# 33 instead of 30 seven-product sets in the down projection of a hybrid decoder layer, with other places for its sums and PSUM banks

## The chip, the cores and the metric

The kernel runs on one core of a Trainium2 chip. The metric is the device time of one execution in microseconds. Times "by the median" are those of the runs without a profile; the profile is of one further execution, whose own time is given beside its span. TensorE (PE) multiplies, VectorE (DVE) and ScalarE (ACT) work on tiles, SyncE (SP) issues most transfers, GpSimd (POOL) some early ones.

## The reference

One decoder layer on 256 tokens of width 2048: a norm, one input projection into attention heads and pooling channels, both mixers, an output projection with a residual, a second norm, and a gated MLP of hidden width 5632. All of it is float32. The part that matters here is the last product:

```python
gate, val = jnp.split(y, 2, axis=-1)
return (jax.nn.silu(gate) * val) @ w_down
```

`silu(gate) * val` has 256 x 5632 elements (44 blocks of 128 along the hidden width), `w_down` is 5632 x 2048, and the result is added to the residual x.

## The kernel before

**Precision.** Every float32 factor is split into a high part `wh` (rounded to the fp32r type by ScalarE, line 180) and a low part `wl` (what is left, `raw - wh`, by VectorE, line 186). A product of two split factors is three matmuls: high by high, high by low, low by high.

**Rows.** All weights come as a list of rows (`rows`, from `plan`). A row is one transfer into a `raw` tile of up to 128 x 2048, a high part and a low part. The rows are used in the order of the list; the steps of the program, u, are the halves of a row, or whole rows of the two special kinds below. At the first step of a row c the program issues, in this order: the high part of row c + 3 (ScalarE), the low part of row c + 2 (VectorE), a `make` if one is due, work set for this step by `later`, work that the step before left in `deferred`, and then the matmuls of row c. Each engine works strictly in the order in which its instructions are issued. `raw` tiles rotate over five buffers, `wh` over four, `wl` over three. When the low part of a row is done its `raw` tile is free, and the transfer five places further on in the list is issued on SP's queue.

**MLP stages.** The MLP is done in three thirds of the hidden width (`THIRDS`: 8, 8 and 6 pairs of 128 x 2 hidden channels). In each third an up stage makes the hidden values, a gate block and a value block of 16 half rows together for every pair, and then a down stage multiplies them by `w_down`. A down stage has two runs, nb = 0 and nb = 1, one for each half of the 2048 output columns. A run goes over the pairs j of its third. For one pair the product is a 2 x 2 block product: two halves of the tokens, two blocks of hidden channels, two blocks of 512 columns.

**Plain rows and sets.** A pair is done in one of two ways. In the plain way (`eight_products`) it takes one row of 2048 columns and 8 products, 24 matmuls of 128x512. As a set of seven products (Strassen's scheme in Winograd's form) it takes two rows: a *mixed* row of four blocks that are sums of weight blocks (`seven_mixed`, 4 products, 12 matmuls), and a *rest* row of three blocks (`seven_rest`, 3 products, 9 matmuls). `SEVEN` names the pairs of each run that are sets. For a mixed row, `make` (lines 194 to 196) adds blocks of weights on VectorE earlier, in an up stage, and stores the result to DRAM (`mixed`); `EARLY` and `PLACES` say at which rows. The hidden values of a set need sums of their own (`left_sums`, lines 855 to 858), which are made once per pair and third.

**PSUM.** A run uses all eight banks: two tiles of two banks (`twos`, tag `acc`), and two pairs of single banks (`ones_`, tags `aux` and `small`). Four banks hold the results c(t, b) of token half t and column block b; four hold the products p1, p5, p6 and p7 of the sets, summed over all sets of the run. When the last set's rest row has been multiplied, ScalarE copies p1 (line 897), and at the next step VectorE makes the closing sums of the sets, `seven_sums`: lines 905, 906, 908 and 910 read the p banks, and three further additions (lines 913 to 915) work in SBUF alone. `done` (line 970) adds the c banks to x; in the last third it also sets the stores to `out`. In a plain row that closes a run, the low part that is due is held back until the first token half is done (`hold`).

**The end of an up stage.** The last value block's results are evacuated (lines 531, 534, 788), go through the convolution on ScalarE (lines 798 and 800), the taps on VectorE (line 806), the product with the gate (line 831), the high part of the hidden values (line 832) and, one row later, their low part (line 846). This tail lies in the first rows of the down stage.

Of the kernel before, what the change touches and what calls it, by code (L numbers as in the profile page):

```python
# [26 lines left out]
OP = mybir.AluOpType  # L27
# [24 lines left out]
OK = (0, 4, 12, 8)  # L52
WOFF = ((32, 32), (16, 36))
THIRDS = ((0, 8), (8, 16), (16, 22))
SEVEN = (((1, 2, 3, 4, 5, 6), (1, 2, 3, 4, 5)), 2 * ((1, 2, 3, 4, 5, 6),), ((1, 2, 3, 4), (1, 2, 3)))
EARLY = (37, 38, 40, 42, 44)
PLACES = ((2, 3, 4, 5, 6, 7), (0, 0.5, 1, 1.5, 2, 3, 4, 4.5, 5, 6, 6.5, 7), (0, 0.5, 1, 1.5, 2, 3, 4))


def out_order(blocks, pools):  # L60
# [5 lines left out]
def plan():  # L66

    rows = [(k, i) for i, k in enumerate(24 * ["tok"] + 25 * ["feat"])]
    makes, t = list(EARLY), 0
    for (g0, g1), sevens, places in zip(THIRDS, SEVEN, PLACES):  # L70
        c = rows[-1][1] + 1
# [23 lines left out]
def layer(ctx: ExitStack, tc: tile.TileContext, xT, wts, mix, par, rel_d, ident_d, icnt_d, out):  # L95
    nc = tc.nc
# [355 lines left out]
    def store(xd, queue):  # L452
        x, d = xd
        queue.dma_start(d, x.rearrange("p j n b -> p (j n b)"))
# [138 lines left out]
    def later(n, f):  # L593
        agenda.setdefault(now[0] + n, []).append(f)
# [266 lines left out]
    def product(ps, left, right, first, last):  # L861
        (ah, al), (wh, wl) = left, right
        for n, (a, w) in enumerate(((ah, wh), (ah, wl), (al, wh))):
            nc.tensor.matmul(ps, a, w, start=(first and n == 0), stop=(last and n == 2), skip_group_check=True)  # L864
# [5 lines left out]
    def seven_mixed(u, j, run, first):  # L870

        c = where[u][0]
        t3, t1, t2, t4 = quarters(c)
        del wparts[c]
        s2, s3, _, s1 = (tuple(late["S", j][:, a, i, :] for a in range(2)) for i in range(4))
        a22 = tuple(late["hid"][:, 2 * j + 1, a, P:] for a in range(2))
        p1, p5, p6, p7 = run["p"]
        product(p5, s1, t1, first, False)
        product(p6, s2, t2, first, False)
        product(p7, s3, t3, first, False)  # L880
        product(run["c"][1][0], a22, t4, (1, 0) in run["left"], False)

    def seven_rest(u, j, run, first, last):

# [15 lines left out]
    def seven_sums(run, a):  # L900

        x2, c = late["x2"], run["x2"]
        _, p5, p6, p7 = run.pop("p")
        b = scratch("sb").rearrange("p a n -> p (a n)")
        nc.vector.tensor_tensor(b, a, p6, op=OP.subtract)
        nc.vector.tensor_tensor(c(0, 0), a, c(0, 0), op=OP.add)
        d = scratch("sd").rearrange("p a n -> p (a n)")
        nc.vector.tensor_tensor(d, b, p7, op=OP.add)
        second = x2[:, :, run["n"] + 512:run["n"] + 1024]
        nc.vector.tensor_tensor(second, second, p5[:, None, :].to_broadcast([P, 2, 512]), op=OP.subtract)  # L910

        def rest():
            nc.vector.tensor_tensor(c(0, 1), c(0, 1), b, op=OP.subtract)
            nc.vector.tensor_tensor(c(1, 0), d, c(1, 0), op=OP.add)
            nc.vector.tensor_tensor(c(1, 1), c(1, 1), d, op=OP.subtract)
        if run["end"]:
            rest()
        else:
            later(2, rest)

    def eight_products(u, j, run, fresh, last, final):

# [22 lines left out]

    for n, ((g0, g1), sevens) in enumerate(zip(THIRDS, SEVEN)):
        ups = []
        for g in range(g0, g1):
            ups.append(feat_block(lambda: late["h"], XK, lambda ps, g=g: gate(ps, g)))
            ups.append(feat_block(lambda: late["h"], XK,  # L950
                                  lambda ps, g=g, j=g - g0, sevens=sevens, end=g == g1 - 1: value(ps, g, j, j in sevens[0], end)))
        u0 = len(steps)
        steps += [h for b in ups for h in b]
        if n == 0:
            for q in range(4):
                after(u0 + 2 + 3 * q, lambda q=q: x2_turn(q))
        for nb in range(2):
            run = {"n": nb * 1024, "end": n == 2 and nb == 1}

            def done(t, lo, m, run=run, n=n, nb=nb):  # L960
                x2 = late["x2"][:, t, run["n"] + lo:run["n"] + lo + m]
                c, acc_ = run["c"][t], run["acc"][t]
                if acc_ is not None and m == 1024:
                    parts = [(acc_.rearrange("p a n -> p (a n)"), x2)]
                elif m == 1024:
                    parts = [(c[b], x2[:, b * 512:(b + 1) * 512]) for b in range(2)]
                else:
                    parts = [(c[lo // 512], x2)]
                for ps, x in parts:
                    nc.vector.tensor_tensor(x, ps, x, op=OP.add)  # L970
                if n == 2:
                    k = min(m, 768 - lo) if nb and t else m
                    store = lambda: nc.sync.dma_start(out[:, t, run["n"] + lo:run["n"] + lo + k], x2[:, :k])
                    store() if nb else later(2, store)

            run["done"] = done
            run["x2"] = lambda t, b, run=run: late["x2"][:, t, run["n"] + b * 512:run["n"] + (b + 1) * 512]
            fresh0 = {(t, b) for t in range(NT) for b in range(2)}
            for j in range(g1 - g0):
                def chunk(u, j=j, nb=nb, run=run, sevens=sevens[nb], size=g1 - g0, fresh0=fresh0, end=n == 2 and nb == 1):  # L980
                    if j == 0:
                        run["left"] = set(fresh0)
                        pair = [acc("ps_down") for _ in range(2)]
                        ones_ = [[f("ps_down") for f in (aux, small)] for _ in range(2)]
                        twos = [[t[:, b, :] for b in range(2)] for t in pair]
                        if nb:
                            run["c"], run["acc"], p = [twos[1], ones_[0]], (pair[1], None), [twos[0], ones_[1]]
                        else:
                            run["c"], run["acc"], p = ones_, (None, None), twos[::-1]
                        run["p"] = p[0][0], p[1][1], p[0][1], p[1][0]  # L990
                        run["spare"] = p[0][0]
                    if j in sevens:
                        seven_mixed(u, j, run, j == sevens[0])
                    else:
                        eight_products(u, j, run, run["left"], j == size - 1, end and j == size - 1)
                        run["left"] = set()
                if j == g1 - g0 - 1:
                    hold.add(len(steps))
                steps.append([chunk])
                steps.append([lambda u, j=j, run=run, sevens=sevens[nb]: j in sevens and  # L1000
                              seven_rest(u, j, run, j == sevens[0], j == sevens[-1])])
# [3 lines left out]
    n = len(steps)  # L1005
# [113 lines left out]
```

## Time and profile before

| | us |
|---|---|
| median of 3 runs | 988.18 (987.61 to 988.70) |
| profiled execution | 989.15, its span 987.1 |
| first down stage | 458.3 to 538.6 of the span |
| second up stage | 538.6 to 712.7 |
| second down stage | 712.7 to 791.7 |
| third up stage | 791.7 to 922.3 |
| third down stage | 922.3 to 982.8 |

Columns of a timeline: start, length (of the whole group where a count over 1 ends the row), engine, line, operation, result <- operands, shape, count, and in brackets the idle time before it with what ended it. The length of a matmul row is longer than the distance to the next one, because matmuls are pipelined. The table of windows gives for each stretch its length and the busy time of PE, PEld, DVE, ACT and POOL, then the clock granted to TensorE, the share of the DMA engines and GB/s. The chain of waits gives start, length and the work that the end of the program hung on.

### The profile page before, as it was taken

How to read it: one execution, taken by the hardware profiler on the slowest of the kernel's cores; microseconds unless marked ns; L12 is line 12 of the kernel's file. 1: busy time of each engine (PE TensorE's matmuls, PEld its weight loads, DVE VectorE, ACT ScalarE, POOL GpSimd, SP SyncE). 2: the span in 40 equal slices, each digit the busy share in tenths (PEclk: the TensorE clock that was granted, in tenths of full speed). 3: DMA queues.
4: the chain of work that ended last, by engine and by line, in shares of the span. 5: the costliest groups of instructions: out<-in, count | busy, mean ns of one | idle time of the engine just before them, and what ended most of it. 6: DMA issues, size and time to landing. Idle time of an engine off the chain costs nothing.

```text
span 987.1 us, 13541 instructions
## 1 busy us (share of the span) xinstructions
PE 981.3 (99%) x5270; PEld 848.9 (86%) x5270; DVE 849.6 (86%) x912; ACT 618.5 (63%) x726; POOL 61.3 (6%) x118
## 2 busy tenths in 40 slices
PE   9999999999999999999999999999999999999998
PEld 7888888898888888888878888888888888888886
DVE  6776859888888998998898889999989899998897
ACT  6654446454557766776755567766775746766752
POOL 0302322200002310000000000000000000000000
PEclk9999999999999999999999999999999999999999
DMA  9959775689878898776978889878988988977483
GB/s 349 315 215 299 247 244 203 208 327 357 333 266 306 291 330 337 268 274 248 369 277 355 318 337 397 316 282 325 363 320 327 398 312 350 368 300 272 170 320 139
DMA packets 49551, 296.88 MB, mean 301 GB/s; under 512 B 6776, under 2 KB 9464, under 8 KB 19024
## 3 DMA queue, kind: packets, MB, share of 16 engines
q1 hardware_dynamic: 44800, 284.09, 76.3%
q0 software_dynamic: 4688, 11.94, 4.1%
q8 instruction: 41, 0.67, 0.3%
q14 instruction: 22, 0.18, 0.0%
HBM read 256.28 MB, written 39.72 MB: 300 GB/s over the span
## 4 chain that ended last, share of the span: by engine, by line
PE 96%; DMA 1%; DVE 1%; ACT 0%; issue 0%; SPq 0%; DVEq 0%; ACTq 0%
PE ps_feat L262 41%; PE ps_feat L264 21%; PE ps_down L864 20%; PE ps_tok L250 9%; PE ps_val L240 4%; DMA raw<-in_wts 1%; PE ps_pool L271 1%; PE ps_s L483 1%; DVE wl L186 1%; PE ps_av L519 0%; DVE x L970 0%; ACT wh L180 0%; PE ps_av L521 0%; PE ps_val L231 0%; DVE x L910 0%
## 5 line engine op out<-in xcount | busy, mean ns | idle before, releaser
L262 PE MATMUL ps_feat<-x2h,wh 128*128 128x512 f32 x1406 | 478.2, 389 | 0.0
L186 DVE TENSOR_TENSOR wl<-raw,wh 128x2048 fp32r<-128x2048 f32 (+1 forms) x175 | 381.5, 2194 | 23.1 <-ACT wh L180 16.0
L180 ACT ACTIVATE wh<-raw 128x2048 fp32r<-128x2048 f32 (+1 forms) x175 | 321.5, 1844 | 123.4 <-DMA raw<-in_wts 63.3
L264 PE MATMUL ps_feat<-x2h,wl 128*128 128x256 f32 x1408 | 388.6, 276 | 0.0
L262 PEld LDWEIGHTS ps_feat<-x2h,wh 128*128 128x128 f32 x1406 | 263.9, 188 | 54.9
L264 PEld LDWEIGHTS ps_feat<-x2h,wl 128*128 128x128 f32 x1408 | 264.3, 188 | 0.0
L864 PE MATMUL ps_down<-wh,hid 128*128 128x512 f32 (+1 forms) x408 | 131.0, 387 | 0.0
L158 DVE TENSOR_TENSOR wl<-raw,wh 128x2048 fp32r<-128x2048 f32 (+3 forms) x44 | 83.0, 1895 | 37.8 <-ACT wh L157 29.4
L531 ACT ACTIVATE fs<-ps_feat 128x512 f32<-128x512 f32 x52 | 31.0, 596 | 109.6 <-PE ps_feat L264 85.4
L864 PEld LDWEIGHTS ps_down<-wh,hid 128*128 128x128 f32 x408 | 76.4, 188 | 15.8
L262 PE MATMUL ps_feat<-cat,wh 128*128 128x512 f32 x256 | 87.3, 389 | 0.0
L250 PE MATMUL ps_tok<-wh,xh 128*128 128x512 f32 x256 | 80.1, 391 | 0.0
L864 PE MATMUL ps_down<-wh,sums 128*128 128x512 f32 x240 | 79.8, 389 | 0.0
L800 ACT ACTIVATE z<-u,pv 128x256 f32<-128x256 f32 x176 | 79.0, 498 | 0.0
L864 PE MATMUL ps_down<-wl,hid 128*128 128x512 f32 (+1 forms) x204 | 79.0, 387 | 0.0
L157 ACT ACTIVATE wh<-raw 128x2048 fp32r<-128x2048 f32 (+3 forms) x44 | 69.3, 1598 | 10.6 <-DMA raw<-in_wts 7.6
L264 PE MATMUL ps_feat<-cat,wl 128*128 128x256 f32 x256 | 70.7, 276 | 0.0
L806 DVE TENSOR_TENSOR y<-y,z 128x512 f32<-128x512 f32 x88 | 60.6, 689 | 8.6 <-ACT z L800 4.0
L534 DVE TENSOR_TENSOR fs<-ps_feat,fs 128x512 f32<-128x512 f32 x52 | 35.8, 689 | 31.9 <-ACT fs L531 31.7
L250 PEld LDWEIGHTS ps_tok<-wh,xh 128*128 128x128 f32 x256 | 48.1, 188 | 10.0
L262 PEld LDWEIGHTS ps_feat<-cat,wh 128*128 128x128 f32 x256 | 48.1, 188 | 10.0
L864 PEld LDWEIGHTS ps_down<-wh,sums 128*128 128x128 f32 x240 | 45.1, 188 | 9.4
(184 smaller groups left out, 1048.8 us busy)
## 6 DMA issues: line engine op xcount, KB each, us to landing
raw<-in_wts SPq DMA_DIRECT2D x148, 1024.0 KB, 7.5
raw<-in_mix SPq DMA_DIRECT2D x30, 1024.0 KB, 6.1
mixed<-raw SPq DMA_DIRECT2D x30, 1024.0 KB, 7.7
raw<-mixed SPq DMA_DIRECT2D x30, 1024.0 KB, 7.0
raw<-in_wts SPq DMA_DIRECT2D x30, 768.0 KB, 6.0
raw<-in_wts SPq DMA_DIRECT2D x4, 512.0 KB, 7.1
x2d<-x2x POOLq DMA_DIRECT2D x4, 512.0 KB, 6.9
x<-x2d POOLq DMA_DIRECT2D x32, 64.0 KB, 6.5
```

The costliest lines, as they stand in the source:

```text
L157: nc.scalar.activation(wh, w, AF.Copy)
L158: nc.vector.tensor_tensor(wl, w, wh.bitcast(F32), op=OP.subtract)
L180: nc.scalar.activation(w, raws[c][:, :width(c)], AF.Copy)
L186: nc.vector.tensor_tensor(wl, raws[c][:, :width(c)], wh.bitcast(F32), op=OP.subtract)
L240: nc.tensor.matmul(ps[b][:, t, :], xh[:, k, a, ts], w[:, ws], start=False, stop=(k == KT - 1 and n == 2), skip_group_check=True)
L250: nc.tensor.matmul(ps[:, t, :], act[:, k0 + k, a, ts], w[:, ws], start=(first and k == 0 and n == 0), stop=(last and k == 1 and n == 2))
L262: nc.tensor.matmul(ps, wh[:, ws], act[:, k, :, :], start=(bool(first) and n == 0), stop=False, skip_group_check=True)
L264: nc.tensor.matmul(ps[:, S:], wl[:, ws], act[:, k, 0, :], start=False, stop=(last and n == len(ks) - 1), skip_group_check=True)
L534: nc.vector.tensor_tensor(dst, ps[:, :, :S], dst, op=OP.add)
L800: nc.scalar.activation(z[i][:, m, :], u[:, m, 1 - i:1 - i + S], AF.Copy, scale=cw[1 - i])
L806: nc.vector.tensor_tensor(y, y, t, op=OP.add)
L864: nc.tensor.matmul(ps, a, w, start=(first and n == 0), stop=(last and n == 2), skip_group_check=True)
```

## The change

Three more pairs are done as sets: pair 6 of the second run of the first third, and pair 0 of both runs of the last third. So the last third's runs now begin with a set. `PLACES` gives the makes of the three new mixed rows: two more in the first up stage, and one more in the last. In `seven_mixed` the product p5 is the last of the four, not the first. The three additions of `seven_sums` are set singly, at distances of 2, 4 and 6 steps after the second run and 4, 6 and 8 after the first one, instead of all three after 2. The stores of the last third's first run are set 9 steps on instead of 2, behind the last of these additions. The p and c banks are dealt out in another way: in a first run p1 and p5 lie in the second of the two-bank tiles and p6 and p7 in the first; in a second run p1 and p5 lie in single banks.

```diff
-SEVEN = (((1, 2, 3, 4, 5, 6), (1, 2, 3, 4, 5)), 2 * ((1, 2, 3, 4, 5, 6),), ((1, 2, 3, 4), (1, 2, 3)))
+SEVEN = (2 * ((1, 2, 3, 4, 5, 6),), 2 * ((1, 2, 3, 4, 5, 6),), ((0, 1, 2, 3, 4), (0, 1, 2, 3)))
-PLACES = ((2, 3, 4, 5, 6, 7), (0, 0.5, 1, 1.5, 2, 3, 4, 4.5, 5, 6, 6.5, 7), (0, 0.5, 1, 1.5, 2, 3, 4))
+PLACES = ((2, 3, 4, 4.5, 5, 6, 6.5, 7), (0, 0.5, 1, 1.5, 2, 3, 4, 4.5, 5, 6, 6.5, 7), (0, 0.5, 1, 1.5, 2, 3, 4, 5))
...
         p1, p5, p6, p7 = run["p"]
-        product(p5, s1, t1, first, False)
         product(p6, s2, t2, first, False)
         product(p7, s3, t3, first, False)
         product(run["c"][1][0], a22, t4, (1, 0) in run["left"], False)
+        product(p5, s1, t1, first, False)
...
-        def rest():
-            nc.vector.tensor_tensor(c(0, 1), c(0, 1), b, op=OP.subtract)
-            nc.vector.tensor_tensor(c(1, 0), d, c(1, 0), op=OP.add)
-            nc.vector.tensor_tensor(c(1, 1), c(1, 1), d, op=OP.subtract)
-        if run["end"]:
-            rest()
-        else:
-            later(2, rest)
+        adds = [lambda: nc.vector.tensor_tensor(c(0, 1), c(0, 1), b, op=OP.subtract),
+                lambda: nc.vector.tensor_tensor(c(1, 0), d, c(1, 0), op=OP.add),
+                lambda: nc.vector.tensor_tensor(c(1, 1), c(1, 1), d, op=OP.subtract)]
+        for i, f in enumerate(adds):
+            f() if run["end"] else later((2 if run["n"] else 4) + 2 * i, f)
...
-                    store() if nb else later(2, store)
+                    store() if nb else later(9, store)
...
                         if nb:
                             run["c"], run["acc"], p = [twos[1], ones_[0]], (pair[1], None), [twos[0], ones_[1]]
                         else:
-                            run["c"], run["acc"], p = ones_, (None, None), twos[::-1]
-                        run["p"] = p[0][0], p[1][1], p[0][1], p[1][0]
+                            run["c"], run["acc"], p = ones_, (None, None), twos
+                        run["p"] = p[1][1], p[1][0], p[0][0], p[0][1]
```

## The prediction

> **What bounds the kernel now.** I read the busy table first, then the chain of waits in order of time, then the timelines of VectorE and ScalarE around the places that the change touches.
>
> ```profile
> PE 981.3 (99%) x5270; PEld 848.9 (86%) x5270; DVE 849.6 (86%) x912; ACT 618.5 (63%) x726; POOL 61.3 (6%) x118
> ...
> PE 96%; DMA 1%; DVE 1%; ACT 0%; issue 0%; SPq 0%; DVEq 0%; ACTq 0%
> ```
>
> ```profile
> 458.42 49.53 PE ps_down L864 x218
> 507.98 0.69 DVE wl L186
> 508.72 30.03 PE ps_down L864 x131
> ...
> 712.87 78.94 PE ps_down L864 x348
> ```
>
> TensorE sets the time: it is busy in 99% of the span and is 96% of the chain. The down stages are one unbroken run of L864 matmuls, except for one wait on VectorE at 507.98. So a removed matmul is worth its pitch, 78.94 / 348 = 0.2268 us, and any new wait of TensorE counts in full. The reader should see that there is nothing else to gain here and much to lose.
>
> **The change part by part.** *Matmuls.* A plain row has 24, a set 12 + 9 = 21. Three more sets remove 9 x 0.2268 = **-2.04 us**. The Trainium skill ("TensorE: Matmul & The Clock Gate", Part 1) gives N / 2.4 GHz + 2.5 ns, 215.8 ns for 512 columns; by it the term would be an estimated -1.94. The trace's pitch is longer, and I use the trace.
>
> *What each set adds elsewhere.* Three makes (L194 to L196), three splits of a rest row, one set of left sums (pair 0 of the third stage; the first stage already made those of pair 6), and per set 1024 KB read, written and read again, plus 768 KB instead of 1024.
>
> ```profile
> L194 DVE TENSOR_TENSOR raw<-raw 128x1024 f32<-128x1024 f32 x30 | 36.6, 1218 | 0.6 <-DMA raw<-in_mix 0.6
> L195 DVE TENSOR_TENSOR raw<-raw 128x512 f32<-128x512 f32 x30 | 20.8, 693 | 1.0
> L855 DVE TENSOR_TENSOR y<-y 128x128 f32<-128x128 f32 x64 | 18.7, 292 | 2.2
> ```
>
> ```profile
> 458.30:538.60 80.30, 79.97 (x354) 65.70 (x353) 71.02 (x53) 52.64 (x39) 0.00 (x0) 1.00 0.83 322
> ...
> 791.70:922.30 130.60, 130.60 (x771) 115.53 (x770) 117.82 (x124) 86.23 (x114) 0.00 (x0) 1.00 0.80 307
> ```
>
> A make is 1.22 + 2 x 0.69 = 2.6 us of VectorE, left sums about 4 x 0.29 + 0.69 = 1.9. In the third up stage (last row: span 130.60, VectorE 117.82, DMA share 0.80) this gives 122.3 of 130.6: it fits, so I cost it at nothing. If that cover were gone, the low parts would be late there, as below. The first up stage has the same matmuls per row and only two more makes. The transfers I also cost at nothing in the up stages; in the down stages they lengthen landings (rival 2).
>
> *The start of the third down stage: the new burst.* Until now its first row was plain (5.44 us of matmuls), which covered the last value block's tail on VectorE and ScalarE. Now pair 0 is a set, so a low part is due every 2.4 us from the first row on. Before, with the first matmul of the stage at 922.25 as zero of t:
>
> ```profile
> 922.25 0.40 PE L864 MATMUL ps_down<-wh,hid 128*128 128x512 f32 x1
> ```
>
> ```profile
> 923.08 0.69 DVE L534 TENSOR_TENSOR fs<-ps_feat,fs 128x512 f32<-128x512 f32 x1 [1.75 <-ACT fs L531]
> 923.81 0.69 DVE L788 TENSOR_TENSOR u<-fs,rrow 128x512 f32<-128x512 f32 x1
> 924.41 0.69 DVE L858 TENSOR_TENSOR sums<-y,sums 128x512 fp32r<-128x512 f32 x1
> 925.02 1.75 DVE L186 TENSOR_TENSOR wl<-raw,wh 128x1536 fp32r<-128x1536 f32 x1
> 928.10 1.49 DVE L806 TENSOR_TENSOR y<-y,z 128x512 f32<-128x512 f32 x2 [1.34 <-ACT z L800]
> 929.63 0.69 DVE L831 TENSOR_TENSOR y<-y 128x512 f32<-128x512 f32 x1
> 930.24 2.28 DVE L186 TENSOR_TENSOR wl<-raw,wh 128x2048 fp32r<-128x2048 f32 x1
> 932.44 0.69 DVE L846 TENSOR_TENSOR hid<-y,hid 128x512 fp32r<-128x512 f32 x1
> ```
>
> ```profile
> 923.98 1.91 ACT L180 ACTIVATE wh<-raw 128x2048 fp32r<-128x2048 f32 x1
> 925.79 0.58 ACT L798 ACTIVATE y<-u,pv 128x256 f32<-128x256 f32 x1
> ...
> 930.41 0.63 ACT L832 ACTIVATE hid<-y 128x512 fp32r<-128x512 f32 x1 [1.94 <-DVE y L831]
> 930.95 8.00 ACT L180 ACTIVATE wh<-raw 128x1536 fp32r<-128x1536 f32 x5
> ```
>
> VectorE takes in this order: tail sums, one low part, the taps (which wait for ScalarE's convolution), the product L831, the next low part. That second low part, of pair 2's mixed row, ended at t = 10.27, and TensorE came to that row at 5.44 + 4.76 = 10.20 (its second matmul, the first to need wl, 0.23 later): just in time. The order is that of the program and stays.
>
> ```profile
> L180 ACT ACTIVATE wh<-raw 128x1536 fp32r<-128x1536 f32 x30 | 44.6, 1486 | 13.4 <-PE ps_down L864 10.6 <-DMA raw<-in_wts 2.2
> ```
>
> After: the first low part is pair 1's mixed row, 2.77 to 5.06; due 4.76 + 0.23 = 4.99, wait 0.1 with the hand-over. ScalarE's high part at 1.73 is a rest row, 1.49 us instead of 1.91, so the convolution and taps come 0.42 earlier: taps 5.43, L831 to 7.65, the next low part 7.57 to 9.32. It is pair 1's **rest** row, due at 4.76 + 2.72 + 0.1 + 0.23 = 7.81: wait 9.37 - 7.81 = 1.56. The row after needs ScalarE again: L832 7.74 to 8.37, then the high part of pair 2's mixed row 8.28 to 10.2, its low part 10.25 to 12.5. TensorE gets there at 11.18 (+ 0.23): wait 1.14. From there VectorE (1.75 + 2.28, less overlap, per 4.76 us) keeps ahead. Sum **+2.8 us**; bounds 2.4 to 3.0 (each hand-over within 0.1, taps as measured).
>
> *The change of column halves.* The banks that the second run starts on come free by the last sums of the first.
>
> ```profile
> 495.25 0.69 DVE L905 TENSOR_TENSOR sb<-sa,ps_down 128x512 f32<-128x512 f32 x1 [0.64 <-ACT sa L897]
> ...
> 497.18 1.21 DVE L910 TENSOR_TENSOR x<-x,ps_down 128x1024 f32<-128x1024 f32 x1
> ...
> 504.57 0.68 DVE L913 TENSOR_TENSOR x<-x,sb 128x512 f32<-128x512 f32 x1
> ```
>
> ```profile
> 747.73 0.69 DVE L905 TENSOR_TENSOR sb<-sa,ps_down 128x512 f32<-128x512 f32 x1 [0.64 <-ACT sa L897]
> ...
> 749.66 1.21 DVE L910 TENSOR_TENSOR x<-x,ps_down 128x1024 f32<-128x1024 f32 x1
> ```
>
> ```profile
> 948.72 0.69 DVE L905 TENSOR_TENSOR sb<-sa,ps_down 128x512 f32<-128x512 f32 x1 [0.97 <-ACT sa L897]
> ...
> 951.78 1.28 DVE L970 TENSOR_TENSOR x<-ps_down,x 128x512 f32<-128x512 f32 x2
> 952.98 2.28 DVE L186 TENSOR_TENSOR wl<-raw,wh 128x2048 fp32r<-128x2048 f32 x1
> 955.18 1.28 DVE L970 TENSOR_TENSOR x<-ps_down,x 128x512 f32<-128x512 f32 x2
> ```
>
> In stages one and two the second run starts with a plain row into the pair of banks that now holds p1 and p5. So it waits for L910, the fourth sum, where it waited for L905. By counts of 0.2268 us that start is at 458.42 + 174 x 0.2268 = 497.9 (497.75 by the matmul's own row) in stage one and 712.87 + 174 x 0.2268 = 752.3 in stage two. L910 ended 498.39 and 750.87: a wait of 0.5 to 0.7 in stage one if its sums are as late as before, none if they are as early as in stage two. I take the middle, **+0.35** (0 to 0.7). Singly issued additions take 1.8 us (L913 to L915) from ahead of the low parts behind 504.57, so the wait at 507.98 (0.69 in the chain, of which one matmul's 0.23 was work) goes: **-0.5**. Placed at +4, +6, +8 steps, each delays one low part by 0.6, which the two-row lead hides.
>
> In stage three the second run now starts with a set. Its fourth product (p5) goes to the bank that the first run's c(1,0) leaves, which is read by the last L970 pair. L905 to the end of that pair's first add: 955.18 + 0.69 - 948.72 = 7.15 us; the held low part is now a rest row, 0.53 shorter: 6.62. p5 is due 2.04 after the run's end (three products). The run's end is 922.25 + 132 x 0.2268 = 952.2. L905 stood 3.5 us ahead of it here, 2.6 in stage one, 4.6 in stage two; 6.62 - 2.04 - that gives waits of 1.1, 2.0 and 0. I take **+0.9**, a little below this stage's own, because TensorE, late by 2.8, gives the loads time.
>
> *The tail.*
>
> ```profile
> 971.70 1.92 ACT L180 ACTIVATE wh<-raw 128x2048 fp32r<-128x2048 f32 x1 [4.44 <-DMA raw<-in_wts]
> ```
>
> ```profile
> 982.77 0.28 PE L864 MATMUL ps_down<-wh,hid 128*128 128x256 f32 x1
> ```
>
> ```profile
> 983.36 0.42 DVE L939 TENSOR_TENSOR x<-ps_down,x 128x256 f32<-128x256 f32 x1
> ```
>
> The last load came late, the closing sums ran late, and L939 began 0.3 behind the last matmul. Two output stores that were issued ahead of that load now stand seven steps later, behind it: **-0.2** (0 to -0.25).
>
> Sum: -2.04 - 0.5 - 0.2 + 0.35 + 2.8 + 0.9 = **+1.3 us**. The profiled execution took 989.15 (span 987.1 and 2.05 around it), 0.97 above the median of 988.18; like for like 990.45, and by the median **989.5 us**, +0.13%. Below 0.2% (2.0 us) a measurement of this kernel can hardly tell from no change.
>
> **The rivals.** *1. The burst is absorbed.* Nothing waits at the start of stage three or at its column change: -2.04 - 0.5 - 0.2, 985.4 us. For it: stage two runs six sets on end twice without one wait. Against: there too the first row is plain, and the low part behind the taps has 0.2 us in hand; a rest row in its place is due 2.6 earlier.
>
> *2. Landings, not the order, decide* (the slower side). A raw buffer is loaded five rows ahead, when its low part is done; landing, high part and low part must fit in five rows, 5 x 2.38 = 11.9 us of sets. With 1.92 + 2.29 of work 7.7 us are left for the landing.
>
> ```profile
> 490.00:495.00 5.00, 5.00 (x23) 4.14 (x23) 2.88 (x2) 4.10 (x3) 0.00 (x0) 1.00 1.02 428
> ```
>
> ```profile
> raw<-in_wts SPq DMA_DIRECT2D x148, 1024.0 KB, 7.5
> ```
>
> ```profile
> raw<-in_wts SPq DMA_DIRECT2D x2, 1024.0 KB, 9.5
> ```
>
> The median just fits, but at the end of stage one's six sets the DMA share is 1.02, and the two 1024 KB weight loads issued between 475 and 500 us landed in 9.5 (last row, of that window alone). Above some 8 us the plain row that closes stage three's first run waits too (1 us at 9) and the column change takes its upper 2.0; with 0.7 in stage one: -2.74 + 2.8 + 1.0 + 2.0 + 0.7 = +3.8, 992.0 us; with half of the excess over the forecast, 990.7. Against: five sets there, not six, and TensorE held up before.
>
> *3. The clock.* A wait of TensorE might lower its granted clock. The row above shows 1.00, and after the wait at 507.98 the pitch is 30.03 / 131 = 0.229. The Trainium skill (same page, Part 1, "The HAM clock gate") states that an idle window of about 3.4 us halves the clock until another such window is busy. The waits of 1.56 and 1.14, with 2 us of matmuls between, are shorter than that; if they counted as idle, 3.4 us of work would take twice as long: an estimate of +3.4, 992.9 us. No run here shows it.
>
> **How the numbers follow.** Forecast (both new waits, 988.0 to 991.0): 0.58, of which 0.08 lies beyond +2.0 us. Rival 1: 0.12. Rival 2: 0.27, of which 0.03 stays within 2.0. Rival 3: 0.03. Faster 0.12, same 0.50 + 0.03 = 0.53, slower 0.08 + 0.24 + 0.03 = 0.35. The range, 986.3 to 991.8, leaves out rival 1 (0.12) and the dearer part of 2 and 3 (0.08).
>
> **What would show it.** L864 matmuls: nine fewer, and in stage three two TensorE waits on wl (L186) within the first 12 us, the larger behind L831; then one on an L970 add 2 us into the second run. No wait near 508. If the first two are missing, the order of VectorE is not what I read, and rival 1 holds. If ScalarE waits long for raw (DMA) in the middle of stage three, and TensorE behind it, rival 2 holds. Matmul pitches near 0.45 us would be rival 3.

## The result, and the profile after

The kernel after the change takes **994.37 us** (median of 12 runs, 991.61 to 1001.05); the kernel before, run beside it, 988.47 (12 runs). The ratio is 1.0057, with a 95% interval of 1.0038 to 1.0076. So three sets more made it slower by 0.6%, and the time lies above the predicted range, 986.3 to 991.8. Of most kernels below, the one before among them, an execution now and then took some 8 us longer (5 of the 112 of the kernel before, 13 of the 30 of e5 to e8); these widen the intervals.

The profiled execution after the change took 995.21 us, its span 993.4, against 989.15 and 987.1 before. The first rows to read are the busy table's (busy us, share of the span, instructions):

```profile
PE 982.5 (99%) x5261; PEld 849.0 (85%) x5261; DVE 864.6 (87%) x929; ACT 624.6 (63%) x730; POOL 60.9 (6%) x118
```

Nine matmuls fewer, 15 us more of VectorE, and TensorE still "99% busy". A busy share can't show where 6 us come from. The windows can. Each stretch below runs from the first matmul of a stage to the first of the next (length, then busy time of PE, PEld, DVE, ACT, POOL; granted clock, DMA share, GB/s). After the change:

```profile
458.31:541.03 82.72, 80.81 (x350) 66.39 (x349) 72.76 (x54) 56.22 (x43) 0.00 (x0) 0.98 0.92 351
541.03:715.15 174.12, 174.12 (x1026) 154.00 (x1025) 162.05 (x175) 116.92 (x156) 0.00 (x0) 1.00 0.88 329
715.15:795.51 80.36, 79.20 (x350) 65.25 (x349) 73.03 (x54) 54.59 (x41) 0.00 (x0) 1.00 0.89 347
795.51:926.11 130.60, 130.60 (x770) 115.76 (x769) 121.15 (x132) 86.90 (x115) 0.00 (x0) 1.00 0.85 321
926.11:988.87 62.76, 60.25 (x268) 48.87 (x267) 57.03 (x47) 36.39 (x30) 0.00 (x0) 1.00 0.66 239
```

The three down stages before:

```profile
458.26:538.59 80.33, 80.00 (x354) 65.73 (x353) 71.01 (x53) 52.64 (x39) 0.00 (x0) 1.00 0.83 322
712.71:791.64 78.93, 78.93 (x350) 65.28 (x349) 70.71 (x52) 54.07 (x40) 0.00 (x0) 1.00 0.90 353
922.25:982.77 60.52, 60.52 (x274) 50.26 (x273) 52.71 (x45) 33.28 (x28) 0.00 (x0) 1.00 0.60 216
```

The up stages are as long as before. The down stages grew by 2.39, 1.43 and 2.24 us; with 0.05 ahead of them and 0.2 behind the last matmul that is the whole 6.3 us of span. The second stage is the surprise: no set was added there. The first has one set more and so three matmuls fewer, which should have made it shorter, and its clock column reads 0.98.

TensorE's timeline in the first stage after the change (start, length, engine, line, operation; in brackets the idle time and what ended it):

```profile
468.09 0.39 PE L864 MATMUL ps_down<-wl,sums 128*128 128x512 f32 x1
468.31 0.61 PE L864 MATMUL ps_down<-wh,sums 128*128 128x512 f32 x2
470.85 0.73 PE L864 MATMUL ps_down<-wl,sums 128*128 128x512 f32 x1 [1.92 <-DVE wl L186]
471.38 1.05 PE L864 MATMUL ps_down<-wh,sums 128*128 128x512 f32 x2
472.23 0.63 PE L864 MATMUL ps_down<-wl,sums 128*128 128x512 f32 x1
472.66 0.63 PE L864 MATMUL ps_down<-wh,sums 128*128 128x512 f32 x1
473.08 0.63 PE L864 MATMUL ps_down<-wh,hid 128*128 128x512 f32 x1
...
474.36 0.40 PE L864 MATMUL ps_down<-wh,sums 128*128 128x512 f32 x1
474.60 0.39 PE L864 MATMUL ps_down<-wl,sums 128*128 128x512 f32 x1
```

Two things show. At pair 2's mixed row, the fourth row of the stage (some of the expectations below call it the third), TensorE stands 1.92 us for a low part. The two matmuls of the second line start at 468.31 and 0.23 later, so by starts the next one comes 2.1 us late (470.85 - 468.54 - 0.23). Behind it the starts are 0.43 us apart instead of 0.23, until 474.36: the clock is halved for 3.5 us, which costs 1.7. The same row waits in the second stage, at full clock:

```profile
726.93 0.50 PE L864 MATMUL ps_down<-wl,sums 128*128 128x512 f32 x1 [1.16 <-DVE wl L186]
```

In the third stage the waits are those that were forecast:

```profile
935.48 0.50 PE L864 MATMUL ps_down<-wl,hid 128*128 128x512 f32 x1 [1.24 <-DVE wl L186]
...
938.66 0.50 PE L864 MATMUL ps_down<-wl,sums 128*128 128x512 f32 x1 [0.84 <-DVE wl L186]
...
960.91 0.50 PE L864 MATMUL ps_down<-wh,sums 128*128 128x512 f32 x1 [0.42 <-DVE x L967]
```

The wait near 508 is gone.

**Where the lateness begins.** Followed back from 470.85, each step late by the one ahead of it: VectorE's low part at 468.51, the taps, the tail's sums at 460.75 (1.66 later than before, the stage beginning at the same time), a low part that waits for ScalarE, and there:

```profile
454.28 1.92 ACT L180 ACTIVATE wh<-raw 128x2048 fp32r<-128x2048 f32 x1 [4.16 <-DMA raw<-mixed]
```

ScalarE stands 4.2 us for the first mixed row's load. Before, the same instruction began at 449.04 without a wait. The load was not slow, it was issued late. SP's own queue after the change:

```profile
437.02 0.33 SPq L197 DMA_DIRECT2D mixed<-raw x1
447.35 0.33 SPq L149 DMA_DIRECT2D raw<-mixed x1
447.73 0.42 SPq L197 DMA_DIRECT2D mixed<-raw x1
448.20 0.42 SPq L149 DMA_DIRECT2D raw<-in_wts x1
```

For 10.3 us SP issues nothing, and then four transfers at once. In the middle of a program whose transfers fill the DMA engines to 0.9, they lie idle:

```profile
444.00:446.00 2.00, 2.00 (x14) 1.76 (x13) 1.97 (x3) 1.53 (x1) 0.00 (x0) 1.00 0.01 4
446.00:448.00 2.00, 2.00 (x13) 1.77 (x12) 1.93 (x2) 0.00 (x0) 0.00 (x0) 1.00 0.00 0
```

What it stood for is read from VectorE: the load starts 0.03 us after this low part is done.

```profile
445.04 2.28 DVE L186 TENSOR_TENSOR wl<-raw,wh 128x2048 fp32r<-128x2048 f32 x1
```

That is not the row whose buffer I took the load to have, but the next one. The reason is in a function that the diff doesn't touch:

```python
turn_of[0] += 1
if turn_of[0] % (RAWS + 1) == 1:
    return late["pool"].tile([P, CH], F32, name="raw", tag="raw")
return wpool.tile([P, CH], F32, name="raw", tag="raw", bufs=RAWS)
```

The five `raw` buffers are not one ring. Every fifth tile, rows and makes counted alike, takes a buffer of its own; the others rotate over four. By the addresses that the built program gives its tiles, which no trace shows, nearly all loads take the buffer of the load three to five places back. But where the fifth turn falls on a row between two makes that are one row apart, a load takes the buffer of the load only two places back, which is freed a whole row later; and all that stands behind it on SP waits too. By these addresses this happened nowhere before the change. After it, it happens twice: to the first mixed row's load (447.35), and in the second up stage, where SP stands from 584.32 to 596.30, ScalarE then waits 5.16, 3.23 and 3.94 us for loads, and VectorE, busy in 162 of that stage's 174 us, hasn't caught up when the second down stage begins. The added makes have shifted the turn. The traces show the two stands of SP and, for the first, the low part that ended it.

**The theory**, then: stages one and two lose 5.2 us (2.1 of wait and 1.7 of clock, then 1.4) to the order in which buffers come free, not to the work that was added. **The rival**: the added makes and transfers are too much for the up stages.

### The profile page after: what moved, and what is told of

Same layout as the page of the kernel before. It is cut to its first block, busy times and chain, and to the rows that moved or that the text cites. A ratio compares the mean times of both kernels' runs of the same rounds, so it can differ in the third digit from the quotient of the medians.

```text
span 993.4 us, 13571 instructions
## 1 busy us (share of the span) xinstructions
PE 982.5 (99%) x5261; PEld 849.0 (85%) x5261; DVE 864.6 (87%) x929; ACT 624.6 (63%) x730; POOL 60.9 (6%) x118
## 5 line engine op out<-in xcount | busy, mean ns | idle before, releaser
L180 ACT ACTIVATE wh<-raw 128x2048 fp32r<-128x2048 f32 (+1 forms) x178 | 326.5, 1839 | 137.6 <-DMA raw<-in_wts 66.8
L186 DVE TENSOR_TENSOR wl<-raw,wh 128x2048 fp32r<-128x2048 f32 (+1 forms) x178 | 387.6, 2186 | 19.5 <-ACT wh L180 10.3
L864 PE MATMUL ps_down<-wh,hid 128*128 128x512 f32 (+1 forms) x378 | 127.9, 388 | 0.0
L864 PE MATMUL ps_down<-wh,sums 128*128 128x512 f32 x264 | 93.8, 392 | 0.4 <-DVE x L967 0.4
L864 PEld LDWEIGHTS ps_down<-wh,hid 128*128 128x128 f32 x378 | 71.0, 189 | 14.7
L157 ACT ACTIVATE wh<-raw 128x2048 fp32r<-128x2048 f32 (+3 forms) x44 | 69.3, 1598 | 10.7 <-DMA raw<-in_wts 7.4
L864 PE MATMUL ps_down<-wl,hid 128*128 128x512 f32 (+1 forms) x189 | 73.5, 389 | 1.2 <-DVE wl L186 1.2
L864 PEld LDWEIGHTS ps_down<-wh,sums 128*128 128x128 f32 x264 | 50.1, 190 | 11.2 <-DVE x L967 0.8
```

Of the source, the lines that this page charges most:

```text
L157: nc.scalar.activation(wh, w, AF.Copy)
L180: nc.scalar.activation(w, raws[c][:, :width(c)], AF.Copy)
L186: nc.vector.tensor_tensor(wl, raws[c][:, :width(c)], wh.bitcast(F32), op=OP.subtract)
```

## The experiments

The times of each stage below are of one profiled execution, from its first matmul to the first of what follows. Ratios are against the runs of the kernel before on the same chip; they follow the means, so that a single long execution moves them more than it moves the median (e12).

| run | sets | median us | ratio (95%) | stage 1 | stage 2 | stage 3 |
|---|---|---|---|---|---|---|
| before | 30 | 988.47 | | 80.33 | 78.93 | 60.52 |
| after | 33 | 994.37 | 1.0057 (1.0038 to 1.0076) | 82.72 | 80.36 | 62.76 |
| e1_tail_later | 33 | 989.93 | 1.0011 (0.9994 to 1.0028) | 78.98 | 78.91 | 62.35 |
| e2_first_only | 31 | 989.93 | 1.0023 (1.0008 to 1.0038) | 81.15 | 78.94 | 60.52 |
| e3_third_only | 32 | 992.16 | 1.0032 (1.0020 to 1.0044) | 79.62 | 80.35 | 62.24 |
| e4_before_tail | 30 | 988.07 | 1.0002 (0.9983 to 1.0020) | 79.78 | 78.90 | 60.50 |
| e5_phase2 | 33 | 998.08 | 1.0108 (1.0068 to 1.0149) | 78.92 | 78.94 | 62.69 |
| e6_before_phase1 | 30 | 1005.15 | 1.0140 (1.0101 to 1.0180) | 79.64 | 80.44 | 60.53 |
| e7_31_phase2 | 31 | 995.20 | 1.0082 (1.0053 to 1.0112) | 78.94 | 78.93 | 60.52 |
| e8_31_phase2_sums | 31 | 999.62 | 1.0105 (1.0058 to 1.0153) | 78.97 | 78.93 | 60.53 |
| e9_late_phase2 | 33 | 990.80 | 1.0023 (1.0013 to 1.0032) | 78.96 | 78.93 | 62.17 |
| e10_before_late_phase1 | 30 | 989.68 | 1.0017 (1.0008 to 1.0025) | 80.06 | 80.36 | 60.53 |
| e11_31_late_phase2 | 31 | 987.62 | 0.9994 (0.9986 to 1.0003) | 80.15 | 78.94 | 60.50 |
| e12_32_late_phase2 | 32 | 987.41 | 1.0001 (0.9983 to 1.0020) | 78.94 | 78.93 | 59.84 |
| e13_32_tail_later | 32 | 987.40 | 0.9984 (0.9960 to 1.0009) | 78.91 | 78.90 | 59.86 |
| e14_31_one_make_less | 31 | 987.81 | 0.9989 (0.9964 to 1.0013) | 78.93 | 78.93 | 60.54 |

### Which part of the change costs what: e1 to e4

e1 takes the change whole and sets the last value block's tail two steps later, as all other value blocks have it, so that the low part due goes ahead of it; e4 does the same to the kernel before.

```diff
-            if end:
-                rest(parts)
-            else:
-                later(2, lambda: rest(parts))
+            later(2, lambda: rest(parts))
```

> The changed kernel, but the taps, the product and the high part of the last value block are set two steps on instead of at once. Theory A (VectorE's order at the start of a down stage: the low part of the fourth row on stands behind the taps, so any lateness of the up stage becomes a wait of TensorE there): in stages one and two the low part of pair 2's mixed row now comes ahead of the taps with some 2 to 3 us in hand, so the waits there (2.1 us and the half-rate stretch behind it in stage one, 1.4 in stage two) go. In stage three the wait only moves to the rest row of pair 2 and shrinks from 2.6 to about 1.5. Sum: 994.4 - 5 - 1 = about 988, and little spread. Theory B (late landings of the weights alone make the waits, whatever the order): the waits of stages one and two stay within 0.5 us, about 993.

> The kernel before, with the tail of the last value block set two steps on as in the first of these runs. Nothing waits there before, so Theory A expects no change: 988.2 within 0.4, with the margin of pair 2's mixed row up from 0.2 to some 3 us. If the order of the tail mattered in another way (ScalarE's high parts behind it), slower by up to 1.

e1 lost the waits in stages one and two, 4.4 us of the median, though SP's stand ahead of stage one was still there (437.26 to 447.60); the low part no longer queues behind the late tail. The third stage shrank by 0.4 only, where 1.1 was expected, so that the median is 989.93 and not 988. e4 gained nothing that can be told. So in stage one the tail's order turns a late load into a wait of TensorE, but it is not what makes the load late.

e2 has only the new set of the first stage, e3 only those of the third; the makes go with them (in e2 six in the third up stage, in e3 seven in the first).

```diff
-SEVEN = (2 * ((1, 2, 3, 4, 5, 6),), 2 * ((1, 2, 3, 4, 5, 6),), ((0, 1, 2, 3, 4), (0, 1, 2, 3)))
+SEVEN = (2 * ((1, 2, 3, 4, 5, 6),), 2 * ((1, 2, 3, 4, 5, 6),), ((1, 2, 3, 4), (1, 2, 3)))
```

```diff
-SEVEN = (2 * ((1, 2, 3, 4, 5, 6),), 2 * ((1, 2, 3, 4, 5, 6),), ((0, 1, 2, 3, 4), (0, 1, 2, 3)))
+SEVEN = (((1, 2, 3, 4, 5, 6), (1, 2, 3, 4, 5)), 2 * ((1, 2, 3, 4, 5, 6),), ((0, 1, 2, 3, 4), (0, 1, 2, 3)))
```

> The changed kernel with pair 0 of the last third plain again in both runs (31 sets; the makes of the first up stage as in the changed kernel, six in the third). Theory A: stage three goes back to no wait, worth 2.6 + 0.7 of waits less 1.36 of matmuls, so 1.9 below the changed kernel: about 992.5, with the waits at pair 2 of stages one and two still there. Theory B': the two new sets of stage three are the whole loss: about 987.5.

> The changed kernel with the first third as before (11 sets, one make fewer at 6.5 in its up stage, seven in all); the last third has its two new sets. Theory A: stage one starts without a wait as before, stage two too if its lateness came from stage one; the wait near the third set of stage one's second run may come back in part. Stage three keeps 2.6 + 0.7 of waits: before + 3.3 - 1.36 = about 990.2. If stage two still waits at pair 2 (its up stage alone is too full), 991.6. Theory C (DMA jitter anywhere in the program): stage one waits as well, 993 and a wide spread.

e2 keeps the wait of stage one and loses those of two and three; its median, 989.93, is neither of the two that were expected (992.5 and 987.5). That stage two is undisturbed here limits the theory. Up to the end of that stage e2 runs the program of the kernel after, and its SP stands in the second up stage as well:

```profile
582.68 0.33 SPq L197 DMA_DIRECT2D mixed<-raw x1
593.37 0.33 SPq L149 DMA_DIRECT2D raw<-in_wts x1
```

So it does in e1 (580.81 to 590.55). In both, VectorE has caught up when the second down stage begins: the tail's first sum starts 0.8 us into the stage, as in the kernel before, and not 2.3 as in the kernel after. This stand alone thus does not make the wait of stage two. In the kernel after it was longer, 12.0 us against 10.7 and 9.7, and by SP's waits 6.9 us of it were for a load to land, against 4.7 and 3.2. How much of the 1.4 us of stage two in the kernel after is owed to the stand, and how much to that landing, stays open.

e3 is the odd one, at 992.16 above both of its expected times (990.2 and 991.6): with fewer makes in the first up stage, stage one is undisturbed, but the second stage, to which it adds no set, waits 1.4 us. By the addresses, in e3 the turn falls so that the first mixed row of the *second* stage takes the buffer two places back, and SP stands from 692.37 to 702.71. That is the place of the stand ahead of stage one in the kernel after, a stage later. It fits the theory, and hardly an account of work added.

### The same work with another turn: e5 to e11

If the turn is the cause, it can be moved without any other edit. e5 (33 sets), e6 (the kernel before) and e7 (31 sets) start the count elsewhere: at 2, 1 and 2. By the addresses, e5 and e7 then have no load that takes a buffer two places back, and e6 has one at the end of the second up stage, where SP stands from 699.84 to 710.18.

```diff
-    late, turn_of = {}, [0]
+    late, turn_of = {}, [2]
```

> The kernel after the change with the turn of the raw buffers begun two later, so that the buffer from the other pool falls on other rows; the same 33 sets, the same instructions. Theory A (the order in which raw buffers come free): no load has to wait for the buffer of a row whose low part comes a whole row later, so the new waits at the third row of the first and second down stages (2.1 and 1.4 us) and the halved clock behind the first (1.8 us) are gone, and the third stage keeps its 2.6 + 0.7: 994.4 - 5.3 = 989.1 us (988.6 to 989.9). Rival B (the added makes take too much of VectorE or of the transfers in the up stages): the waits stay, 993 to 995 us. Rival C (the halved clock is what counts, by itself): 992.5.

> The kernel before the change with the turn of the raw buffers begun one later; 30 sets, nothing else. Theory A: the load of the second down stage's first mixed row now takes the buffer of a row that is freed a row later, SP's queue stands some 10 us near 692 us, and TensorE waits about 1.4 us at the third row of the second down stage: 988.5 + 1.4 = 989.9 us (989.2 to 990.4), without a single set added. Rival B (added work is what makes the first and second stage wait): as before, 988.5 us.

> The third stage's pair 0 left plain as before the change, pair 6 of the first stage's second run a set (31 sets), the other parts of the change kept, and the turn of the raw buffers begun two later. Theory A: one set less three matmuls (-0.68 us) and no wait near 508 (-0.5 us), no wait at the start of any down stage: 987.3 us (986.8 to 987.8), under both kernels. Rival B: as the same 31 sets without the other turn, 989.9 us.

The medians are all far too long, and the stages all as theory A has them: 78.92 and 78.94 for e5, 80.44 in e6's second stage. What was added lies ahead of them, where the fifth buffer comes into use. TensorE's timeline of e5:

```profile
241.29 0.28 PE L264 MATMUL ps_feat<-cat,wl 128*128 128x256 f32 x1
242.70 0.51 PE L262 MATMUL ps_feat<-cat,wh 128*128 128x512 f32 x1 [1.13 <-DVE fs L534]
247.08 0.58 PE L264 MATMUL ps_feat<-cat,wl 128*128 128x256 f32 x1 [3.87 <-DVE wl L186]
247.45 0.63 PE L262 MATMUL ps_feat<-cat,wh 128*128 128x512 f32 x1
```

Waits of 1.13 and 3.87 us with their restarts, 5.4 in all, then a halved clock until 252, 2.4 more. If all of e5's executions lose these 7.8 us, its 998.08 would be 990.3 without them. By their medians these runs settle nothing. e9 to e11 are the same three with the turn moved at the 24th tile instead, behind that place:

```diff
-        turn_of[0] += 1
+        turn_of[0] += 3 if turn_of[0] == 24 else 1
```

(e10: 2 for 3.)

> The same 33 sets as after the change; the turn of the raw buffers is moved on by two, but only once, at its 24th turn (in the first up stage), so that the place near 241 us, where the runs with the turn begun later lost 7 to 8 us, stays as it was. Theory A (the order in which raw buffers come free): no wait at the third row of the first and second down stages and no halved clock behind it, 994.4 - 5.3 = 989.1 us (988.6 to 989.9), with the third stage's 2.6 + 0.7 still there. Rival B (the added makes themselves): 993 to 995 us.

> The kernel before the change, 30 sets, with the turn of the raw buffers moved on by one at its 24th turn. Theory A: TensorE waits some 1.4 to 1.6 us at the third row of the second down stage and nowhere new besides, 988.5 + 1.5 = 990.0 us (989.4 to 990.6). Rival B: as before, 988.5 us.

> 31 sets (pair 6 of the first stage's second run added, pair 0 of the third stage plain), the other parts of the change kept, the turn moved on by two at its 24th turn. Theory A: -0.68 us of matmuls, -0.5 us for the wait near 508, no new wait: 987.3 us (986.8 to 987.8), faster than both kernels. Rival B: 989.9 us, as the same sets without the other turn.

**e10 is the proof** that the turn alone can do it. It is the kernel before, with 30 sets and the same instructions, and it is slower by 0.17% (0.08 to 0.25%), 989.68 us where 990.0 was expected. Its second stage takes 80.36 us instead of 78.93. SP stands from 691.39 to 701.73, where in the kernel before the load was issued at 697.00; it is the stand ahead of stage one in the kernel after, of 10.3 us there too, at the same place of the next stage. (That stage two of the kernel after also took 80.36 is chance: its stand lay far ahead.) The chain of waits shows the whole way (start, length, what); parts are left out:

```profile
699.42 2.30 DVE wl L186
701.71 0.02 issue
701.73 6.77 DMA raw<-mixed
708.50 0.02 issue
708.52 1.92 ACT wh L180
...
722.12 2.29 DVE wl L186
724.41 0.04 issue
724.46 35.65 PE ps_down L864 x156
```

The chain runs from the low part that frees the buffer to the late load, and over ScalarE's high part, the tail and the next low part to the matmul. SP stands once more in e10, in the middle of the third up stage (836.32 to 846.13), and no wait follows (60.53). Held in the middle of an up stage, a load need cost nothing; held at the first mixed row of a down stage, it cost a wait in every profiled execution that has the tail as before (stage one of the kernel after and of e2, stage two of e3, e6 and e10). In e9, the change whole with the turn repaired, SP issues the same load at 443.23, and stages one and two take 78.96 and 78.93: both waits and the halved clock are gone. The median fell by 3.6 us, to 990.80, not by the 5.4 of the two profiled spans, and lies above the 988.6 to 989.9 expected. One reason is in the runs of the kernel after: the clock is not halved in all of them (below). The wait of stage two need not be in all of them either, as e1 and e2 show. The profiled execution of e9 is its fastest, 989.73; what the others add isn't traced.

e8 sets the last three additions of `seven_sums` (the folding additions) at once again, as before the change (in e7's kernel).

```diff
-        for i, f in enumerate(adds):
-            f() if run["end"] else later((2 if run["n"] else 4) + 2 * i, f)
+        if run["end"]:
+            for f in adds:
+                f()
+        else:
+            later(2, lambda: [f() for f in adds])
```

> As the run of 31 sets with the turn begun two later, but the three folding additions set all at once two steps on, as before the change. If the single additions are what took away the wait near 508, it comes back: +0.5 us (0.2 to 0.7) over that run, with TensorE waiting on a low part some 6 us into the second run of the first stage; in the second stage nothing. Rival (the first run's end and its banks took it away): no difference.

The wait near 508 did not come back (stage one 78.97, against 78.94 for e7). In e10, by contrast, with the banks and sums of before, TensorE still loses 0.4 us there. So the single additions aren't what removed it. Nor need it be any part of the change: e4 and e6 have the sets, banks and sums of before too, and their stage one takes 79.78 and 79.64, where its 351 matmuls alone make 79.6 (351 x 0.2268). The wait comes and goes without the change; on what it hangs is open.

### What is left: e12 to e14

e11 reaches 987.62, where 987.3 was expected, but its profiled run, one of two above 989 among 11, still waits 1.2 us in stage one. No load there takes a buffer two places back, but one was late all the same: SP stands from 393.96 to 403.51, by its waits 9.2 us for the store of a make to land (6.6 in e9), and ScalarE then waits 3.25 us for a load. e14 takes one make out of the first up stage and puts it into the last; the turn is moved by one more, so that two things differ from e11.

```diff
-PLACES = ((2, 3, 4, 4.5, 5, 6, 6.5, 7), (0, 0.5, 1, 1.5, 2, 3, 4, 4.5, 5, 6, 6.5, 7), (0, 0.5, 1, 2, 3, 4))
+PLACES = ((2, 3, 4, 4.5, 5, 6, 7), (0, 0.5, 1, 1.5, 2, 3, 4, 4.5, 5, 6, 6.5, 7), (0, 0.5, 1, 1.5, 2, 3, 4))
```

> As the run of 31 sets with the turn moved on, but the eighth make of the first up stage (6.5) left out there and one more put into the last up stage, where there were seven before the change; the turn is moved on by three so that no load takes a buffer freed a row later. The profiled run of 31 sets still waited 1.2 us at the third row of the first down stage without any late load. Theory (the makes have used up VectorE's slack there, 1.6 us before, 0 in that run): the wait is gone, 987.3 us and no run over 988.5 but for disturbed ones. Rival (a landing): the wait is there in the profile or in as many runs, 987.6 us.

The row to read is the tail's first sum on VectorE; the idle time in brackets is the slack that VectorE has at the stage's end. In e11 there is none:

```profile
460.86 0.69 DVE L534 TENSOR_TENSOR fs<-ps_feat,fs 128x512 f32<-128x512 f32 x1
```

In e14:

```profile
459.41 0.69 DVE L534 TENSOR_TENSOR fs<-ps_feat,fs 128x512 f32<-128x512 f32 x1 [1.59 <-ACT fs L531]
```

The kernel before, e3 and e10, with six or seven makes in the first up stage, have 1.58 or 1.59 there too; e9 and e13, with eight as e11, have 0.33 and 0.31. So the rival has a part: the eighth make takes VectorE's slack, and a transfer that lands late then shows. It is worth up to 1.2 us in some runs, and little in the median: e14's 987.81 is no better than e11's, and above the 987.3 expected, but only one of its 12 runs lies above 988.2.

e12 is e11 with pair 0 of the third stage's *second* run as a set as well (and its make and hidden sums), so that only the first run begins with a plain row; e13 is e12 with e1's edit.

```diff
-... ((1, 2, 3, 4), (1, 2, 3)))
+... ((1, 2, 3, 4), (0, 1, 2, 3)))
```

> As the run of 31 sets with the turn moved on, and pair 0 of the third stage's second run alone a set as well (32 sets; the first run still begins with a plain row). It tells the two new sets of the third stage apart: its start then has no burst (no 2.6 us), and only the column change can wait on the fourth product's bank. 31 sets' time - 0.68 us of matmuls + 0 to 0.9 us: 986.6 to 987.5 us, with 0.7 of wait 987.3. If the first run's burst is not what costs in the third stage, over 988.5.

> As the run of 32 sets with the turn moved on, and the last value block's pieces of the tail set two steps later, as the other value blocks have them. If what is left of lateness in the first down stage (1.2 us of wait in some runs of the 31 sets) is VectorE behind at the stage's end, this takes it away and steadies the runs: 987.0 us (986.5 to 987.4), lowest run near 986.7. If that lateness comes from landings, no change: 987.4.

The third stage falls to 59.84, below the 60.52 of before by a set's three matmuls, with no wait at its start or at its change of columns. The burst of 2.8 us thus belongs to the set at the head of the first run. e13's chain is unbroken in all three stages (its line numbers are three lower):

```profile
458.57 78.90 PE ps_down L861 x348
...
711.60 78.91 PE ps_down L861 x348
...
921.11 58.56 PE ps_down L861 x258
```

e12 and e13 have the lowest medians, 1.1 us under before; with intervals that reach 1.0020 and 1.0009, neither is shown to be faster than the kernel before. By the median e13 gains nothing on e12 (987.40 and 987.41), so it doesn't tell whether the tail's place matters there.

## Why the prediction was wrong, step by step

**The step that failed** is "What each set adds elsewhere", and in it the sentences that the makes fit, "so I cost it at nothing", and that "the first up stage has the same matmuls per row and only two more makes". It named the price if the cover went ("the low parts would be late there") and then checked the cover by busy time of one stage, VectorE's 122.3 of 130.6. Two things are not in such a sum. The makes take turns of the `raw` buffers, so they move the load that waits a row longer: this cost 2.1 us in stage one with 1.7 of halved clock behind it, as e9 and e10 show. Stage two lost 1.4 more, and that the turn alone did this is not shown: in e1 and e2 a stand of SP at the same place led to no wait. And the slack that counts is the one at the stage's end, where the tail's sums had 1.6 us in hand, less than one make of 2.6; in e11, where it was used up, 1.2 us of wait came behind a store that landed late. I had read that a `raw` tile "is loaded five rows ahead" as true for every tile; the code has two rings.

*Matmuls*, -2.04: right. Nine fewer; e14's stage one is one set and the wait near 508 shorter than before, e12's stage three one set shorter.

*The start of the third down stage*, +2.8: right, also in its instants. The second low part ends 0.06 ahead of the matmul at 935.48 and the third 0.06 ahead of that at 938.66, 9.3 and 12.5 us behind the stage's first matmul at 926.11, as forecast. From start to start TensorE lost 0.2, 1.5 and 1.1 us, 2.84 with the restarts, for 0.1, 1.56 and 1.14.

*The change of column halves*: in stage one +0.35 was forecast and nothing came (0 was in its range). In stage three 0.7 came in the kernel after, on an L967 addition two us into the run as forecast, for 0.9; but in e9 it was 0.07. So its size was luck as much as working.

*The wait at 507.98*, -0.5: it went, and e14's stage one puts it at 0.7. But e8 shows that it did not go through the single additions, and e4 and e6 lose it, e4 all but 0.2 us, with the sets, banks and sums of before. The reason was wrong, and that it came out is luck.

*The tail*, -0.2: the last addition came 0.40 behind the start of the last matmul instead of 0.59, as forecast, but the span ended 4.5 us behind that matmul instead of 4.3. The end is the last store's landing, which no term of mine held.

**The sum.** Forecast +1.3; the profiled executions differ by 6.06 us. The terms that were priced come to +1.0 as measured (-2.0 - 0.7 + 2.8 + 0.7 + 0.2); 5.2 more came in stages one and two, where the term stood at nothing. Together that is 6.2 of the span's 6.3.

**The rivals.** The burst was not absorbed. Landings did not decide where rival 2 had them, in stage three and at the column change, nor in stage one: the median landing of a 1024 KB weight row went from 7.5 to 7.7 us, and the late load was late in its issue. In the stand ahead of stage two they had a part. The clock rival was nearest in kind: the clock did halve, but in stage one, behind a wait that I hadn't forecast, and not behind the two of stage three (1.24 and 0.84 us idle).

## What to carry to other kernels

A count of busy time doesn't clear an edit that adds tiles to a rotating pool: work out which earlier tile each new load replaces, and when that one is done, all the more where a queue issues in order and one late buffer holds up everything behind it. Take slack from the rows just ahead of the place that needs it, not from a stage's mean. And when a stage that the edit doesn't touch becomes slower, look for a counter that the edit has shifted; moving only that counter, in the kernel before, is the cheapest test there is.

## What the runs showed of the hardware that was not expected

*The clock.* Behind a wait of 1.92 us TensorE's clock was halved for 3.5 us in the kernel after, and behind one of 1.96 us at the same row in e2 it was not:

```profile
470.81 0.50 PE L864 MATMUL ps_down<-wl,sums 128*128 128x512 f32 x1 [1.96 <-DVE wl L186]
471.14 0.63 PE L864 MATMUL ps_down<-wh,sums 128*128 128x512 f32 x2
471.61 0.39 PE L864 MATMUL ps_down<-wl,sums 128*128 128x512 f32 x1
```

Nor is it the same in every run of one kernel. Of the 12 runs of the kernel after, five list a mean granted clock of 1.000, with a median of 992.3 us, and six one of 0.997 or 0.998, with a median of 994.8. The Trainium skill ("TensorE: Matmul & The Clock Gate", Part 1, "The HAM clock gate") says that a window of about 3.4 us runs free of the kernel, that one idle window halves the clock and one busy window frees it, and gives 426.7 ns for 512 columns at the halved clock. The pitch here, 0.43 us, and the 3.5 us until it was freed agree, and a free-running window would explain why one run is hit and another isn't. The idle time doesn't agree: 1.92 us, little more than half a window, was enough.

*A longer pitch at full clock.* The profiled run of e12 began its first down stage 7.7 us late without any gap. In windows of that execution and of e13's over the same stretch of the first up stage, the first has 1123 matmuls and the second 1167:

```profile
260.00:458.00 198.00, 198.00 (x1123) 171.01 (x1122) 173.92 (x192) 131.76 (x172) 20.65 (x38) 1.00 0.85 311
```

```profile
260.00:458.00 198.00, 198.00 (x1167) 175.22 (x1166) 177.83 (x198) 136.81 (x179) 20.70 (x38) 1.00 0.87 320
```

A pair of matmuls takes 0.353 us there instead of 0.340, with the granted clock at 1.00 in both. The profiled executions of e5, e7 and e8, 1003 to 1007 us long, have it too: 284 or 285 matmuls from 310 to 360 us, as e12 has, and those of e6, e9, before and after have 296. So the four profiled executions that were some 8 us longer than others of their kernel share it; its cause stays open.
